# The order of the FFN's first products, of two heads' products, and of layer 1's modulation in a two-layer diffusion trunk

## The chip, the cores and the metric

The kernel runs on one core of one Trainium2 chip. The metric is the device time of one execution in microseconds. Three runs of the kernel before took 2241.53, 2242.65 and 2244.84 us.

## The reference

One inference step of a trunk with two layers, on 128 context tokens and 512 latent tokens of width 1024, everything in float32. A layer is

```python
mod = silu(cond) @ w_mod + b_mod                       # six vectors of 1024: sh1, sc1, g1, sh2, sc2, g2
h = rms_norm(x) * (1 + sc1) + sh1
a = w_out(merge(neighbourhood attention, grouped-query attention, gated linear attention)(h))
x = x + g1 * a
h = rms_norm(x) * (1 + sc2) + sh2
u = h @ ffn_w_up                                       # 1024 -> 2 x 2816
a, g = split(conv3(u));  x = x + g2 * ((a * silu(g)) @ ffn_w_down)
```

The context tokens use the modulation of `c_ctx`, the latent tokens that of `c`. In the gated linear attention each head's output is a product inside the block plus two products (forward and backward) with the state before the block.

## The kernel before, in words

**Layout.** Activations lie channel-major: a tile is 128 channels by 640 tokens (128 context, 512 latent), and a product runs on halves of 320 tokens (`HT`), called left and right. A float32 product is made of three products of rounded parts, hi·hi, hi·lo and lo·hi, so each operand is split into a hi part (a rounding copy, mostly on ScalarE) and a lo part (a subtraction on VectorE or GpSimd). Weights come from HBM in the order of a plan, through SyncE's queue, and are split in the same way.

**The planner.** The program is a set of Python generators ("streams"). Each yields what it waits for; `Order` keeps an estimated clock for each engine, and always steps the first stream in order of priority that is ready at PE's estimated time, else the one that is ready soonest. So the order of each engine's instructions is fixed when the kernel is built. Priority 0 is for evacuations, factors, splits and weights, 1 for attention and modulation, 2 for the main stream that issues the large products. 

**Buffers.** Most working tiles come from one pool `ub` of 49 tiles of 128×648 (in the mixers four more, which `widen` hands to the weights before the output projection). A stream that asks for a tile waits until one is free. In the FFN the pool holds the factors (28 tiles), two half-tiles `a_hi` and `a_lo` for each finished unit until the part's last down chunk, `up_a`, `up_g` and `cv_a` of the units in work, and `w_last` for each pair of weights in preparation. PSUM gives the products six banks of 512 columns.

**The FFN.** There are 22 units of 128 channels; a unit needs the two up projections a and g. Units 0 and 1 are computed from unnormalised input while the norm is still being made (`raw`, tile `up`). Units 2 to 21 use a seven-product scheme of Strassen's kind over the two halves of tokens and the two up matrices: the normalised input of each of four block pairs gives seven factors, B11 and B21 (right columns), B22 (left), and the differences T1 to T4, each as hi and lo (`factors`). A unit's products go in steps "12" (with B11, B21), "67" (T2, T3), "54" (T1, T4) and "3" (B22), into PSUM tiles pair_x, pair_y and pair_w (`pair_step`); "6" goes into the bank that "1" was read from. `pair_act` adds them up, convolves and gates, and `keep_split` makes a_hi and a_lo.

The down projection runs in five parts of 5, 5, 5, 4 and 3 units (`FFN_PARTS`), each in eight chunks of 128 output channels, "dn". The order of all these steps is made by `ffn_steps`: a part's first chunk is put three steps after the "3" of its last unit (`WAIT`), and then one chunk after each step. A chunk runs one half of the tokens over all units and then the other half (`proj_halves`); each half is evacuated into x with the gate.

**The modulation.** Each of the six vectors is a product of `cT` (32 columns) with 1024×1024 weights, read in 256 KB pieces. `Mod.rest` takes five tiles of `ub`, when eight are free, four of them a ring of two slots; a round loads two blocks of rows (four DMAs, 1 MB), makes eight products of 32 columns by 256, and adds the result to a partial sum. Layer 0's last four vectors run in its mixer, with at least 4000 ns of PE's estimated time between rounds. Layer 1's six vectors, 24 rounds, start when the event `calm` is set, which is at the start of branch b's gates ("gb") in layer 0, at priority 1 and with 2000 ns.

**Gated linear attention.** `gla` is called for two pairs of heads in each layer. Its last products go into one PSUM tile `go`, for each block of 128 tokens and each head: v times At (128 rows), and, but for the context block, two products with the states (64 rows, tiles `S` and `qt`).

Of the kernel before, what the change touches and what calls it, by code (L numbers as in the profile page):

```python
# [9 lines left out]
F32 = mybir.dt.float32  # L10
# [8 lines left out]
P = 128  # L19
D = 1024  # L20
KC = 8
# [243 lines left out]
class Order:  # L265
# [105 lines left out]
def kernel(ctx: ExitStack, tc: tile.TileContext, I, O, depth=2):  # L371
# [358 lines left out]

    class Mod:
        def __init__(self, l, pc=None, ready=None):
            self.l, self.pc, self.ready = l, pc, ready
# [36 lines left out]
            del acc  # L770
            yield from self.finish(ms, pieces, P, 256)

        def rest(self, vectors, after, pause):
# [14 lines left out]
            fetch(0)  # L788
            fetch(1)
            for i in range(0, len(todo), 2):  # L790
                v, k0 = todo[i]
                yield ring[0] + ring[1] + [cT, od.later(pause)]
                acc = yield from TB("mod")
                psum_names.add(acc.ap.tensor.name)
# [4 lines left out]
                yield [acc]  # L799
                if k0 == 0:  # L800
                    act(ms[:, :256], acc[:, :256])
                else:
                    tt(ms[:, :256], acc[:, :256], ms[:, :256], ADD)
                del acc
# [110 lines left out]
        h.done[k].time = od.known[lo.ap.tensor.name]  # L915


    def factors(fa, fb, out, k):

        L, R = slice(0, HT), slice(HT, NT)  # L920
        h1, l1, h2, l2 = yield from ub.several("f_12", 4, 0, F32R)
        b11, b12, b21, b22 = fa[:, R], fa[:, L], fb[:, R], fb[:, L]

        def lo(nm, x, h, l):
            tt(l, x, h.bitcast(F32), SUB, sooner(HT))
            out[nm][k] = (h, l)
            out[nm].ready[k].time = od.known[l.tensor.name]

        yield [fa]
        act(h1[:, L], b11)  # L930
        yield [fb]
        act(h1[:, R], b21)
        act(h2[:, L], b22)
        yield [h1]
        lo("B11", b11, h1[:, L], l1[:, L])
        lo("B21", b21, h1[:, R], l1[:, R])
        yield [h2]
        lo("B22", b22, h2[:, L], l2[:, L])

        yield [fb]  # L940
        tt(b22, b22, b12, SUB)
        tt(b12, b12, b11, SUB)
        tt(b11, b22, b11, ADD)
        tt(b21, b21, b11, SUB)
        yield [fa]
        act(h2[:, R], b12)
        h3 = yield from U("f_hi", F32R)
        act(h3[:, L], b11)
        yield [h2]
        lo("T1", b12, h2[:, R], l2[:, R])  # L950
        l3 = yield from U("f_lo", F32R)
        yield [h3]
        lo("T2", b11, h3[:, L], l3[:, L])
        act(h3[:, R], b21)
        h4 = yield from U("f_34", F32R)
        act(h4[:, L], b22)
        yield [h3]
        lo("T4", b21, h3[:, R], l3[:, R])
        yield [h4]
        lo("T3", b22, h4[:, L], h4[:, R])  # L960
        out.keep += [h1, l1, h2, l2, h3, l3, h4]

    class Factors:
        def __init__(self, nk):
# [26 lines left out]
                   skip_group_check=True)  # L991

    def modulate_factors(x, r, mod, i, offs, out):
        gsc, sh = mod.gsc[:, i], mod.T[:, 24 * i:24 * i + 8]
        cols = [(slice(a, a + n), slice(offs[e], offs[e] + n), e) for e, (a, n) in enumerate(((0, NP), (NP, NS)))]
        for k in range(KC // 2):
            f = []
            for kk in (k, k + KC // 2):
                yield [r, mod.have[12 * i + 4 + kk // 2], mod.have[12 * i + kk // 2]]
                v = yield from U("hv")  # L1000
                eng = sooner(NT)
                for c, o, e in cols:
                    tt(v[:, c], x[kk][:, c], r[:, o], MUL, eng)
                yield [v]
                for c, _, e in cols:
                    act(v[:, c], v[:, c], AF.Identity, scale=gsc[:, kk, e:e + 1], bias=sh[:, kk, e:e + 1])
                f.append(v)
                del v
            od.start(factors(f[0], f[1], out, k), 0)
            del f  # L1010


    def scaled(x, k, ready, mod, i, gh, gl, done):
# [74 lines left out]
    def gla(l, p, q, k, rc, v, zT, zdone, wg, pc, oc, grp):  # L1088
# [198 lines left out]
        for ts_ in ((0,), (1, 2, 3, 4)):  # L1287
# [1 line left out]
            psum_names.add(op.ap.tensor.name)  # L1289
            yield At + qts + [v]  # L1290
            for c, t in enumerate(ts_):
                for h in range(2):
                    r = slice(64 * h, 64 * h + 64)
                    oo = op[r, c * P:(c + 1) * P]
                    mm(oo, v[:, t * P + 64 * h:t * P + 64 * h + 64], At[h][:, t * P:(t + 1) * P], True, t == 0)
                    if t:
                        for e in range(2):
                            mm(oo, sst[e][r, t - 1], qts[e][r, t * P:(t + 1) * P], False, e == 1)
# [387 lines left out]
    def mixer(l, h, pc, wg, raws, full, finish, calm):  # L1686
# [416 lines left out]
        z = yield from pair_act(i, c, pc, ah)  # L2103
        yield from keep_split(i, z, ah, al, have)

    def ffn(l, x, raws, h, pc, mod, ss, nxt, nraws):
        ah, al = {}, {}
        have = [Event() for _ in range(NFF)]
        pairs = {}
# [11 lines left out]
        for step in ffn_steps():  # L2121
# [77 lines left out]
    def program():  # L2199
# [20 lines left out]
        for l in range(depth):  # L2220
# [3 lines left out]
            if l == 0:  # L2224
                yield [h.done[0]]
            if l == 0:
                od.start(mod.rest((2, 3, 4, 5), mod.have[3], 4000.0), 1)
            nxt = None
            if l + 1 < depth:
                nxt = Mod(l + 1)  # L2230
            od.start(next_mod(nxt, calm), 1)
            od.start(spill(x, h.done[KC - 1]), 1)
            full, x = [Event() for _ in range(KC)], [None] * KC

# [21 lines left out]
                ss, nraws = SumSq(), Raw()  # L2256
            else:
                ss = nraws = None
            yield from ffn(l, x, raws, h, pc, mod, ss, nxt, nraws)
            raws = nraws  # L2260
            if nxt is not None:
                mod, pc, wg = nxt, nxt.pc, nxt.wg
# [1 line left out]
    def next_mod(nxt, after):  # L2264
        yield [after]
        if nxt is not None:
            nxt.pc, nxt.wg, nxt.ready, work = load_params(nxt.l)
            od.start(work, 1)
            yield from nxt.rest(range(6), after, 2000.0)

    def spill(x, ready):
        yield [ready]
# [65 lines left out]
```

## Time and profile before

| | |
|---|---|
| median of three runs | 2242.65 us |
| profiled execution, its span | 2246.69 us, 2244.9 us |
| PE busy | 2129.1 us, 95% |
| VectorE (DVE) busy | 1565.5 us, 70% |
| ScalarE (ACT) busy | 1124.9 us, 50% |
| mean granted clock of PE | 0.978 |
| DMA | 209.33 MB, mean 93 GB/s |

The profile is of one execution. A row of the timeline has the start, the time to the end of the last instruction, the engine, the line, the operation, the tile written and the tiles read, and how many instructions it merges; a float32 product with `cT`, `At` or `qt` shows as two instructions, one with rounded operands as one. Products overlap, so the time from one row's start to the next one's start is the better measure of their pace. Layer 0's mixer ends and its FFN begins at 715 us, layer 1 begins at 1178 us, its FFN at 1781 us.

### The profile page before, as it was taken

To read this page: it belongs to the slowest core of one execution; us is meant where nothing else is said; L and a number is where in the kernel's file an instruction comes from. 1 tells how busy PE (TensorE), PEld (TensorE's weight loads), DVE (VectorE), ACT (ScalarE), POOL (GpSimd) and SP (SyncE) were. 2 spreads that over 40 slices of the span, in tenths; PEclk is the share of its full clock that TensorE was granted. 3 is DMA by queue.
4 is the path that set the end of the run, shared out by engine and by line. 5 is a ranking of instruction groups with operands and counts; after the bars stand their busy time and mean duration, and the time that the engine had idled before them with its cause. 6 is when DMAs were issued, how large, how long until landed. Compare 5 with 4: busy or idle time off the path is not lost. (4 is left out here: it accounts for less than half of the span.)

```text
span 2244.9 us, 40057 instructions
## 1 busy us (share of the span) xinstructions
PE 2129.1 (95%) x16208; PEld 2002.3 (89%) x16208; DVE 1565.5 (70%) x2839; ACT 1124.9 (50%) x2067; POOL 222.5 (10%) x284
## 2 busy tenths in 40 slices
PE   6999999999999899999998999999999989999999
PEld 4767989896799789999998889899899978999999
DVE  5375479774247987777876865787655798778785
ACT  4354656552225744454456556565543574445452
POOL 0211110000101000001011110101010200000101
PEclk9998999999999999999999899999999999999999
DMA  9751221126662122222223111211113212222212
GB/s 300 259 189 39 68 80 52 38 72 197 218 205 76 38 73 87 80 78 81 69 83 113 49 51 65 78 53 48 39 49 131 76 38 73 88 85 69 92 62 90
DMA packets 85874, 209.33 MB, mean 93 GB/s; under 512 B 9590, under 2 KB 22518, under 8 KB 85688
## 3 DMA queue, kind: packets, MB, share of 16 engines
q1 hardware_dynamic: 84472, 204.66, 28.0%
q8 instruction: 128, 2.10, 0.4%
q0 software_dynamic: 1216, 2.10, 0.3%
q14 instruction: 58, 0.48, 0.1%
HBM read 197.81 MB, written 10.98 MB: 93 GB/s over the span
## 5 line engine op out<-in xcount | busy, mean ns | idle before, releaser
L445 ACT ACTIVATE w_h<-w_st 128x1024 fp32r<-128x1024 f32 (+4 forms) x292 | 274.3, 942 | 246.7 <-PE dn L436 76.7
L461 DVE TENSOR_TENSOR w_h<-w_st,w_h 128x1024 fp32r<-128x1024 f32 (+4 forms) x248 | 269.0, 1087 | 142.1 <-ACT w_h L445 139.3
L436 PE MATMUL dn<-a_hi,w_h 128*128 128x320 f32 x1408 | 325.6, 313 | 2.4 <-ACT a_hi L445 2.0
L436 PE MATMUL pair_x<-f,w_h 128*128 128x320 f32 x1440 | 232.2, 312 | 23.8 <-ACT f L445 18.1
L436 PEld LDWEIGHTS dn<-a_hi,w_h 128*128 128x128 f32 x1408 | 242.0, 191 | 4.0 <-ACT a_hi L445 4.0
L436 PEld LDWEIGHTS pair_x<-f,w_h 128*128 128x128 f32 x1440 | 217.4, 190 | 27.1 <-ACT f L445 18.6
L436 PE MATMUL dn<-a_lo,w_h 128*128 128x320 f32 x704 | 221.1, 314 | 16.8 <-DVE a_lo L461 16.8
L464 POOL TENSOR_TENSOR w_h<-w_st,w_h 128x1024 fp32r<-128x1024 f32 (+2 forms) x44 | 98.5, 2239 | 746.2 <-ACT w_h L445 585.9
L436 PEld LDWEIGHTS dn<-a_lo,w_h 128*128 128x128 f32 x704 | 134.2, 191 | 19.0 <-DVE a_lo L461 18.7
L473 DVE SCALAR_TENSOR_TENSOR x<-dn,modT,x 128x128 f32<-128x128 f32 (+2 forms) x240 | 97.5, 436 | 53.5 <-PE dn L436 53.1
L436 PE MATMUL gc<-h_hi,w_h 128*128 128x320 f32 x512 | 130.4, 325 | 0.0
L436 PE MATMUL ga<-h_hi,w_h 128*128 128x320 f32 x512 | 128.0, 320 | 0.2 <-ACT sg L445 0.2
L436 PE MATMUL gb<-h_hi,w_h 128*128 128x320 f32 x512 | 128.1, 320 | 0.0
L436 PE MATMUL wo<-m_hi,w_h 128*128 128x320 f32 x768 | 113.8, 310 | 0.0
L436 PEld LDWEIGHTS wo<-m_hi,w_h 128*128 128x128 f32 x768 | 113.1, 188 | 0.4 <-issue 0.4
L436 PEld LDWEIGHTS gb<-h_hi,w_h 128*128 128x128 f32 x512 | 88.9, 189 | 7.5 <-issue 7.5
L436 PEld LDWEIGHTS gc<-h_hi,w_h 128*128 128x128 f32 x512 | 89.9, 192 | 5.2 <-issue 2.0
L436 PEld LDWEIGHTS ga<-h_hi,w_h 128*128 128x128 f32 x512 | 89.6, 191 | 2.9 <-issue 2.4
L445 ACT ACT_TABLE_LOAD x63 | 80.8, 1283 | 10.7 <-PE hss L436 2.7
L436 PE MATMUL gc<-h_lo,w_h 128*128 128x320 f32 x256 | 80.3, 314 | 0.0
L436 PE MATMUL ga<-h_lo,w_h 128*128 128x320 f32 x256 | 79.9, 312 | 0.0
L436 PE MATMUL gb<-h_lo,w_h 128*128 128x320 f32 x256 | 79.6, 311 | 0.0
(411 smaller groups left out, 5328.2 us busy)
## 6 DMA issues: line engine op xcount, KB each, us to landing
w_st<-in_wt_dram SPq DMA_DIRECT2D x204, 512.0 KB, 3.5
mod<-in_w_mod_dram SPq DMA_DIRECT2D x160, 256.0 KB, 4.1
w_st<-in_wt_dram SPq DMA_DIRECT2D x48, 320.0 KB, 2.8
mod_w<-in_w_mod_dram SPq DMA_DIRECT2D x32, 256.0 KB, 6.0
xd<-x SPq DMA_DIRECT2D x16, 320.0 KB, 6.7
x<-xd SPq DMA_DIRECT2D x16, 320.0 KB, 3.0
w_st<-in_wt_dram SPq DMA_DIRECT2D x16, 256.0 KB, 2.6
w_st<-in_wt_dram SPq DMA_DIRECT2D x16, 192.0 KB, 2.3
```

The lines of the kernel that those rows point to most:

```text
L436: nc.tensor.matmul(out, lhsT, rhs, start=start, stop=stop, **kw)
L445: r = nc.scalar.activation(out=out, in_=in_, func=f, **kw)
L461: nc.vector.tensor_tensor(out, a, b, op=op)
L464: nc.gpsimd.tensor_tensor(out, a, b, op=op)
L473: nc.vector.scalar_tensor_tensor(out=out, in0=a, scalar=s, in1=b, op0=op0, op1=op1)
```

## The change

1. `ffn_steps` puts "12" of units 2 and 3 first, then "67" and "54" of unit 2, "67" of unit 3 and "3" of unit 2; from unit 4 on the weave is as it was.
2. `modulate_factors` makes the right columns of all eight blocks and their factors B11 and B21 first (`right_factors`), then the left columns and the other factors (`left_factors`, which makes T3 and T2 before T1 and T4). The blocks' tiles `hv` stay until then.
3. The first down chunk of each part runs both halves for each unit (`proj_whole`), not half after half, and evacuates both at the end.
4. `gla` takes the two heads in turn for each of a block's three products.
5. Layer 1's modulation starts after branch b's attention is done, at priority 3, below the main stream, and without a pause; when part 1 of layer 0's down chunks begins, `hurry` lifts it to priority 1 and gives it a pause of 2000 ns. Its vectors gather in PSUM over eight blocks of rows, and are copied out once.

```diff
@@ ffn_steps
-    for n in range(NRAW, NFF + 1):
-        up, last = n < NFF, n > NRAW
+    a, b = NRAW, NRAW + 1
+    weave += [("12", a), ("12", b), ("67", a), ("54", a), ("67", b), ("3", a)]
+    for n in range(NRAW + 2, NFF + 1):
+        up, last = n < NFF, True
@@ Order
+    def lift(self, gen, prio):
+        for s in self.streams:
+            if s[2] is gen:
+                s[0] = prio
+        self.streams.sort(key=lambda s: s[:2])
@@ Mod.rest
-                yield ring[0] + ring[1] + [cT, od.later(pause)]
-                acc = yield from TB("mod")
+                yield ring[0] + ring[1] + [cT, od.later(self.pause)]
+                if k0 == 0 or not whole:
+                    acc = yield from TB("mod")
...
-                           j == 0, j == 1, tile_position=(0, 32 * g))
+                           k0 + j == a, k0 + j == b, tile_position=(0, 32 * g))
...
+                if not whole or k0 == KC - 2:
+                    yield [acc]
+                    if whole or k0 == 0:
+                        act(ms[:, :256], acc[:, :256])
@@ factors
+    def right_factors(fa, fb, out, k):
+        h, l = yield from ub.several("f_12", 2, 0, F32R)
+        for nm, x, c in (("B11", fa, L), ("B21", fb, R)):
+            yield [x]
+            act(h[:, c], x[:, R])
+            yield [h]
+            factor_lo(out, k, nm, x[:, R], h[:, c], l[:, c])
+        out.keep += [h, l]
+    def left_factors(fa, fb, out, k):
...
+        h2, l2 = yield from ub.several("f_12", 2, 0, F32R)
...
+        out.keep += [h2, l2, h3, l3, h4]
@@ modulate_factors
+        for cols, then in zip(sides, (right_factors, left_factors)):
+            for k in range(KC // 2):
...
+                od.start(then(v[k], v[k + KC // 2], out, k), 0)
+                if then is left_factors:
+                    v[k] = v[k + KC // 2] = None
@@ gla
-                for h in range(2):
-                    r = slice(64 * h, 64 * h + 64)
...
+                for j in range(3 if t else 1):
+                    for h in range(2):
+                        r = slice(64 * h, 64 * h + 64)
+                        oo = op[r, c * P:(c + 1) * P]
+                        if j == 0:
+                            mm(oo, v[:, t * P + 64 * h:t * P + 64 * h + 64], At[h][:, cols], True, t == 0)
+                        else:
+                            mm(oo, sst[j - 1][r, t - 1], qts[j - 1][r, cols], False, j == 2)
@@ mixer
-            if nm == "b":
-                calm.time = 0.0
...
                 if nm == "b" and i == 0:
                     od.start(last.serve(mmb, 4), 0)
+                    calm.time = 0.0
@@ ffn
+                if part == 1:
+                    rush.time = 0.0
...
-                yield from proj_halves(w, a, nb, finish(o, part), "dn")
+                if o:
+                    yield from proj_halves(w, a, nb, finish(o, part), "dn")
+                else:
+                    ps, ev = (yield from proj_whole(w, a, nb, HT, "dn")), finish(o, part)
+                    for hf in range(2):
+                        od.start(ev(hf, ps.pop(0)), 0)
@@ program
-            od.start(next_mod(nxt, calm), 1)
+            lazy = next_mod(nxt, calm)
+            od.start(lazy, 3)
...
+    def hurry(mod, lazy, when):
+        yield [when]
+        mod.pause = 2000.0
+        od.lift(lazy, 1)
```

## Rows read from the trace of the kernel before

**Rows 1.** The page's first part: busy us (share of the span) and instructions by engine.

```profile
PE 2129.1 (95%) x16208; PEld 2002.3 (89%) x16208; DVE 1565.5 (70%) x2839; ACT 1124.9 (50%) x2067; POOL 222.5 (10%) x284
```

**Rows 2.** PE's waits, whole span: waiter, releaser, us in total, times, longest.

```profile
PE pair_x L436 <- ACT f L445: 18.1, 2, 9.0
PE dn L436 <- DVE a_lo L461: 16.8, 8, 2.6
...
PE dn L436 <- ACT a_hi L445: 2.0, 2, 1.0
```

**Rows 3.** PE's timeline, second gla: start us, us, instruction, how many.

```profile
239.18 0.43 PE L436 MATMUL go<-At,vc 128*64 128x128 f32 x2
239.54 0.65 PE L436 MATMUL go<-qt,S 64*64 64x128 f32 x4
240.12 0.43 PE L436 MATMUL go<-At,vc 128*64 128x128 f32 x2
```

**Rows 4.** PE's timeline, first gla.

```profile
185.48 0.69 PE L436 MATMUL go<-At,vc 128*64 128x128 f32 x2
...
187.14 0.69 PE L436 MATMUL go<-At,vc 128*64 128x128 f32 x2
```

**Rows 5.** PE's timeline, one unit of the grouped-query attention.

```profile
401.31 0.44 PE L436 MATMUL g_o<-gp,gcv 128*64 128x128 f32 x4
401.58 1.04 PE L436 MATMUL g_o<-gp,vbT 128*64 128x128 f32 x16
402.56 0.42 PE L436 MATMUL ga<-h_hi,w_h 128*128 128x320 f32 x1
```

**Rows 6.** PE's timeline, waits before first down chunks (in brackets: idle before, releaser).

```profile
820.93 0.63 PE L436 MATMUL dn<-a_lo,w_h 128*128 128x320 f32 x1 [2.61 <-DVE a_lo L461]
...
2173.11 0.42 PE L436 MATMUL dn<-a_lo,w_h 128*128 128x320 f32 x1 [1.39 <-DVE a_lo L461]
```

**Rows 7.** PE's timeline, layer 0's FFN between two parts.

```profile
904.24 1.92 PE L436 MATMUL pair_w<-f,w_h 128*128 128x320 f32 x12
906.00 0.74 PE L436 MATMUL pair_x<-f,w_h 128*128 128x320 f32 x4
```

**Rows 8.** PE's waits between 700 and 860 us.

```profile
PE pair_x L436 <- ACT f L445: 9.0, 1, 9.0
...
PE pair_x L436 <- DVE w_h L461: 1.5, 3, 1.0
PE pair_x L436 <- DVE f L461: 1.3, 1, 1.3
PE dn L436 <- ACT a_hi L445: 1.0, 1, 1.0
```

**Rows 9.** Busy us by stage: window, length, PE, PEld, DVE, ACT, POOL, clock, DMA.

```profile
724.00:821.00 97.00, 81.46 (x529) 79.35 (x527) 92.33 (x166) 64.38 (x117) 7.12 (x14) 0.94 0.18 60
```

**Rows 10.** VectorE's timeline, the in-place differences of one block pair.

```profile
733.54 2.07 DVE L461 TENSOR_TENSOR hv<-hv 128x320 f32<-128x320 f32 x4
```

**Rows 11.** Layer 1's modulation: its instructions (ns min/median/max, first and last start), its stage.

```profile
L436 PE MATMUL mod<-mod,cT x384: 376/379/404, 507.0 to 660.2; 128*32 128x256 f32 x192
L501 SPq DMA_DIRECT2D mod<-in_w_mod_dram x92: 327/366/1021, 507.7 to 653.5; - x92
...
DMA to landing us min/median/max: 2.8/3.9/5.9
...
505.00:665.00 160.00, 38.71 (x396) 13.05 (x396) 7.64 (x18) 2.31 (x6) 0.99 0.66 212
```

**Rows 12.** PE's products of tiles gb and bb in both layers, first and last start.

```profile
L436 PE MATMUL gb<-h_hi,w_h x256: 302/309/616, 505.9 to 649.1; 128*128 128x320 f32 x128
...
L436 PE MATMUL bb<-ob_hi,w_h x128: 304/309/421, 597.6 to 657.4; 128*128 128x320 f32 x128
...
L436 PE MATMUL gb<-h_hi,w_h x256: 302/309/415, 1616.3 to 1717.1; 128*128 128x320 f32 x128
...
L436 PE MATMUL bb<-ob_hi,w_h x128: 303/308/315, 1675.0 to 1724.1; 128*128 128x320 f32 x128
```

More of the change, by code (lines that the diff above doesn't have):

```diff
@@ L732, in __init__ @@
         def __init__(self, l, pc=None, ready=None):
-            self.l, self.pc, self.ready = l, pc, ready
+            self.l, self.pc, self.ready, self.pause = l, pc, ready, 0.0 if l else 4000.0
             self.T = prm.tile([P, 48, 2], F32, tag="modT", bufs=2, name=f"modT{l}")
@@ L771, in first, with rest @@
             yield from self.finish(ms, pieces, P, 256)
-        def rest(self, vectors, after, pause):
+        def rest(self, vectors, after, whole):
             yield [after]
@@ L791, in rest @@
                 v, k0 = todo[i]
-                yield ring[0] + ring[1] + [cT, od.later(pause)]
-                acc = yield from TB("mod")
-                psum_names.add(acc.ap.tensor.name)
+                yield ring[0] + ring[1] + [cT, od.later(self.pause)]
+                if k0 == 0 or not whole:
+                    acc = yield from TB("mod")
+                    psum_names.add(acc.ap.tensor.name)
+                a, b = (0, KC - 1) if whole else (k0, k0 + 1)
                 for j in range(2):
@@ L797, in rest @@
                         mm(acc[32 * g:32 * g + 32, :256], cT[:, k0 + j, :], ring[j][g // 2][:, g % 2 * 256:g % 2 * 256 + 256],
[L798 to L804 removed]
+                           k0 + j == a, k0 + j == b, tile_position=(0, 32 * g))
[4 more added lines that the diff above has]
+                    else:
+                        tt(ms[:, :256], acc[:, :256], ms[:, :256], ADD)
+                    del acc
                 for j in range(2):
@@ L915, in mod_lo @@
         h.done[k].time = od.known[lo.ap.tensor.name]
-    def factors(fa, fb, out, k):
-        L, R = slice(0, HT), slice(HT, NT)
-        h1, l1, h2, l2 = yield from ub.several("f_12", 4, 0, F32R)
-        b11, b12, b21, b22 = fa[:, R], fa[:, L], fb[:, R], fb[:, L]
[L924 to L930, printed above, removed]
+    L, R = slice(0, HT), slice(HT, NT)
@@ new lines, in factor_lo @@
+    def factor_lo(out, k, nm, x, h, l):
+        tt(l, x, h.bitcast(F32), SUB, sooner(HT))
+        out[nm][k] = (h, l)
+        out[nm].ready[k].time = od.known[l.tensor.name]
+    def right_factors(fa, fb, out, k):
[6 more added lines that the diff above has]
+        out.keep += [h, l]
@@ L941, in factors @@
         tt(b22, b22, b12, SUB)
+        h4 = yield from U("f_34", F32R)
+        act(h4[:, L], b22)
         tt(b12, b12, b11, SUB)
         tt(b11, b22, b11, ADD)
-        tt(b21, b21, b11, SUB)
-        yield [fa]
-        act(h2[:, R], b12)
         h3 = yield from U("f_hi", F32R)
         act(h3[:, L], b11)
+        tt(b21, b21, b11, SUB)
+        l3 = yield from U("f_lo", F32R)
+        yield [h4]
+        lo("T3", b22, h4[:, L], h4[:, R])
+        yield [h3]
+        lo("T2", b11, h3[:, L], l3[:, L])
@@ L949, in factors @@
+        act(h2[:, R], b12)
+        act(h3[:, R], b21)
         yield [h2]
         lo("T1", b12, h2[:, R], l2[:, R])
[L951 to L956, printed above, removed]
         yield [h3]
         lo("T4", b21, h3[:, R], l3[:, R])
-        yield [h4]
-        lo("T3", b22, h4[:, L], h4[:, R])
-        out.keep += [h1, l1, h2, l2, h3, l3, h4]
+        out.keep += [h2, l2, h3, l3, h4]
@@ L994, in modulate_factors @@
         gsc, sh = mod.gsc[:, i], mod.T[:, 24 * i:24 * i + 8]
[L995 to L1010, printed above, removed]
+        n = HT - NP
+        sides = (((slice(HT, NT), slice(offs[1] + n, offs[1] + NS), 1),),
+                 ((slice(0, NP), slice(offs[0], offs[0] + NP), 0), (slice(NP, HT), slice(offs[1], offs[1] + n), 1)))
+        v = [None] * KC
+        for cols, then in zip(sides, (right_factors, left_factors)):
+            for k in range(KC // 2):
+                for kk in (k, k + KC // 2):
+                    yield [r, mod.have[12 * i + 4 + kk // 2], mod.have[12 * i + kk // 2]]
+                    if v[kk] is None:
+                        v[kk] = yield from U("hv")
+                    eng = sooner(HT)
+                    for c, o, e in cols:
+                        tt(v[kk][:, c], x[kk][:, c], r[:, o], MUL, eng)
+                    yield [v[kk]]
+                    for c, _, e in cols:
+                        act(v[kk][:, c], v[kk][:, c], AF.Identity, scale=gsc[:, kk, e:e + 1], bias=sh[:, kk, e:e + 1])
+                od.start(then(v[k], v[k + KC // 2], out, k), 0)
+                if then is left_factors:
+                    v[k] = v[k + KC // 2] = None
     def scaled(x, k, ready, mod, i, gh, gl, done):
@@ L1291, in gla @@
             for c, t in enumerate(ts_):
-                for h in range(2):
-                    r = slice(64 * h, 64 * h + 64)
[L1294 to L1298, printed above, removed]
+                cols = slice(t * P, (t + 1) * P)
+                for j in range(3 if t else 1):
[6 more added lines that the diff above has]
+                            mm(oo, sst[j - 1][r, t - 1], qts[j - 1][r, cols], False, j == 2)
             n = P * len(ts_)
@@ L2104, in pair_split, with ffn @@
         yield from keep_split(i, z, ah, al, have)
-    def ffn(l, x, raws, h, pc, mod, ss, nxt, nraws):
+    def ffn(l, x, raws, h, pc, mod, ss, nxt, nraws, rush):
         ah, al = {}, {}
@@ L2142, in ffn @@
                     a = [ah.get(k) for k in ks], [al.get(k) for k in ks]
-                yield from proj_halves(w, a, nb, finish(o, part), "dn")
+                if o:
+                    yield from proj_halves(w, a, nb, finish(o, part), "dn")
+                else:
+                    ps, ev = (yield from proj_whole(w, a, nb, HT, "dn")), finish(o, part)
+                    for hf in range(2):
+                        od.start(ev(hf, ps.pop(0)), 0)
+                    del ps, ev
                 if o == KC - 1:
@@ L2226, in program @@
             if l == 0:
-                od.start(mod.rest((2, 3, 4, 5), mod.have[3], 4000.0), 1)
+                od.start(mod.rest((2, 3, 4, 5), mod.have[3], False), 1)
             nxt = None
@@ L2258, in program @@
                 ss = nraws = None
-            yield from ffn(l, x, raws, h, pc, mod, ss, nxt, nraws)
+            rush = Event()
+            if nxt is not None:
+                od.start(hurry(nxt, lazy, rush), 1)
+            yield from ffn(l, x, raws, h, pc, mod, ss, nxt, nraws, rush)
             raws = nraws
@@ L2268, in next_mod @@
             od.start(work, 1)
-            yield from nxt.rest(range(6), after, 2000.0)
+            yield from nxt.rest(range(6), after, True)
+    def hurry(mod, lazy, when):
+        yield [when]
+        mod.pause = 2000.0
+        od.lift(lazy, 1)
     def spill(x, ready):
```

7 lines of the change are left out of this document (2 added, 5 removed).

## The prediction

> **What bounds the kernel now.** I read the page's busy shares first: TensorE (PE) works 2129.1 of 2244.9 us [rows 1], so a change pays where it shortens PE's own work or one of the waits that make up the other 115.8 us. The view of PE's waits names two that belong to the FFN: the pair products on a factor (18.1 us, two waits) and the down products on the newest half (16.8 and 2.0 us) [rows 2]. I then read PE's timeline at each place that the diff touches, because a busy PE can also work slowly: in the heads' products it does. Last come the stage table around the first FFN's head, for what stands behind its waits, and the views of layer 1's modulation.
>
> **Base of the sum.** The profiled execution took 2246.69 us, 1.8 more than its span; the median shown is 2242.65, 4.0 less. I sum against the execution and take the 4.0 off at the end.
>
> **Heads' turns (gla).** Now a head's three products for one block follow each other, so each accumulates behind the last in the same rows: from one head's At product to the other's is 240.12 − 239.18 = 0.94 us, 1.88 a block [rows 3]. The grouped attention already alternates two heads of the same 128×64 shape: its ten products stand from 401.31 to 402.56, so 0.25 a pair [rows 5]. Three alternated pairs make 0.75 a block, 1.13 less; four blocks with an inter-block part give 4.5 an instance, and three of the four instances run so: 13.6. The first runs at half clock: 187.14 − 185.48 = 1.66 a head, 3.32 a block [rows 4]; at twice 0.75 it saves about 1.8 a block, 7.3, of which I keep 6.4, since the block order is the only thing changed and its wait on qt stays. Together −20. Nothing hides this: PE is the busy engine on both sides. The trace has no two 64-row products of different heads in one PSUM bank, so I bound them by the rows: alternating only the At pairs saves 2×0.36 − 0.25 = 0.47 a block at full clock and about 0.74 at half, −8.6 in all.
>
> On that point a rule speaks against the change. The Trainium skill, page "TensorEngine Tiling (Array Packing)", section "Restrictions and Gotchas", says that different row tiles cannot access one PSUM bank at the same time. Both heads write one bank, though other partitions of it; by the rule only the lower bound would come, −8.6. No row shows the case; it is rival 3.
>
> **First down chunk of each part with both halves.** With the halves in turn, PE has 12 products (0.147 each: 12 in 906.00 − 904.24 = 1.76 us [rows 7]) before it needs the part's last half-tile; with both halves together it has 24, so 1.76 more cover. Eight of the ten parts wait: 3.65 in part 0 of each layer (1.04 on a_hi and 2.61), 1.39 in one, and the other five (16.8 − 2×2.61 − 1.39)/5 = 2.04 [rows 2, 6]. Each loses what the cover reaches: 7×1.76 + 1.39 = −13.7. Bounds: 0, if the half-tile comes later by as much, and the 18.8 of rows 2. It takes two PSUM banks at once of six; three are held by pairs at that point, so I cost it at nothing.
>
> **Right factors and products first.** The first FFN waits 9.0 + 1.3 on unit 2's last factor [rows 8]. The right factors need one column half and no differences, so "12" of units 2 and 3 can follow the raw columns directly, 3.5 us of PE work more before it stands. But VectorE works 92.33 of the 97 us from the first factor to the last half-tile of part 0 [rows 9], and none of its work goes: the four in-place differences of a pair still take 2.07 [rows 10], and each block's first product is cut in three pieces instead of two, eight more instructions a layer. What PE gains early it gives back to VectorE before the first down chunk. At most the idle 4.7 comes back; at worst the eight pieces cost 0.52 each, 4.1. I take −2.5 for each of the two FFNs, −5.
>
> **Layer 1's modulation, taken away where it stood.** It is 24 rounds of eight products; PE is busy with them 38.71 us, 1.61 a round [rows 11]. From the first gb to the last bb layer 0 takes 657.4 − 505.9 = 151.5, layer 1, which has no modulation there, 1724.1 − 1616.3 = 107.8 [rows 12]. The difference and the last round, which stands behind bb, make −45.
>
> **... and put where it goes.** At priority 3 it advances only when nothing else can. Layer 1's same stretch has no PE wait up to the FFN's head, so it will start there: one step takes five tiles of the pool `ub` (if eight are free) and fetches. About ten tiles should be free, the raw columns' sixteen having just come back. Rows 8 show six waits and rows 6 a seventh, the longest good for two rounds, and a tighter pool adds a few: I take ten rounds in waits that are there anyway, at +5 in all (0 to 16).
>
> It keeps the five tiles until its last round. The pool has 49 in the FFN. At step ("67", 7), with part 0's chunks half done, the code must hold 28 factor tiles (7 for each of four block pairs), 10 half-tiles of units 0 to 4 (freed only by the eighth chunk), 2 each of units 5, 6 and 7 (up_a and up_g of unit 7 must exist before "1" is read, which "6" waits for), and unit 7's w_last: 45. With five gone there are 44. So the main stream should stand still there until the modulation has run out, one round after the other, and PE with it; queued behind it are ("67", 7) and everything after, and ScalarE and VectorE run dry. A round then lasts as long as its data: a ring slot is fetched when its half of the products is through, 0.8, two issues of 0.37, landing 3.9 (median) [rows 11], which is 5.4; as the other slot's products overlap a little I take 5.2. Bounds: 4.3 with the shortest landing, 2.8, and 6.4, the spacing they have now ((660.2 − 507.0)/24). Fourteen rounds (9 to 19) make 73, with 3 for products at half clock afterwards: +76 (42 to 125). If the pool is too tight at the head, `hurry` starts it in part 1 and the same count binds in part 2, for about the same price.
>
> The fewer evacuations (18 VectorE additions go) are worth nothing: VectorE has room there.
>
> Sum: −20 − 13.7 − 5 − 45 + 5 + 76 = −2.7; 2246.69 − 2.7 − 4.0 = 2240.0. About what a measurement of this kernel can tell from no change is 0.2%, 4.5 us: the forecast is no change, gains eaten by one standstill.
>
> **Rivals.**
> 1. The five tiles never bind: a unit gets by with fewer, or the modulation takes its tiles so late that no five-unit part follows. For: the last parts hold 8 and 6 half-tiles, 43 or fewer. Against: the count, and 24 rounds need over 100 us. Then the rounds cost 24×1.61 = 38.6 and some 5 of waits on data, less 8 in idle places, +36 instead of +81: 2195.
> 2. Slower: the standstill in part 0 lasts longer, 17 rounds at 6.4, 109 and 3, with 3 for the rest: −83.7 + 115 = +31, 2274. For: rounds now come 6.4 apart, with weights on the same queue. Against: in a standstill nothing else is fetched. It decides from the point where the standstill passes 79 us, 15 rounds at 5.2.
> 3. By the skill's rule the heads overlap in the At pairs alone: 11.4 less gain, 2251. For: no row shows the case. Against: the heads write other partitions.
> 4. The change does not do what it says at the down chunks: VectorE, 92.33 of 97 busy before part 0, shifts the last half-tile with PE, and no cover is gained: 2254. Against: in the parts after it PE alone is full.
>
> **Numbers.** Forecast 0.42, with a range of its own of 2220 to 2262; rival 1 0.28, rival 2 0.16, rival 3 0.08, rival 4 0.06. The forecast's own spread (rounds and their price) is 0.45 below the 0.2% bound, 0.25 within it, 0.30 above. So faster is 0.28 + 0.19 + 0.01 = 0.48; same 0.11 + 0.04 = 0.15; slower 0.37. The range that leaves out two in ten reaches rival 1 below and nearly rival 2 above: 2190 to 2272.
>
> **What would show it.** Right: in gla, pairs of products 0.25 apart and go some 3.5 us long; first chunks waiting under 0.5 us in parts 1 to 3; in layer 0's FFN, between part 0's fifth chunk and its end, a stretch of 60 to 90 us with PE idle on mod loads and nothing else running, at the low one of the two clock levels (1.2 GHz); layer 1's FFN shorter by about 10 us. Wrong: rounds of modulation spread through parts 1 to 3 between full-speed products (rival 1, some 45 us faster), 64-row products still 0.29 apart (rival 3), or an FFN head whose factor wait is gone with VectorE no fuller than now, by which my bound on that edit falls.

## The result: 2256.43 us, 0.6% slower than before

The changed kernel takes 2256.43 us (2252.57 to 2258.47, four runs) against 2242.84 beside it: a ratio of 1.0055, 95% interval 1.0042 to 1.0067. The forecast was 2240, no change. The span of its profiled execution is 2256.7 us, 11.8 more than before. The page after, in its busy shares and in 40 slices of 56 us, shows two places:

```profile
PE 2129.3 (94%) x16208; PEld 1989.5 (88%) x16208; DVE 1564.8 (69%) x2837; ACT 1127.9 (50%) x2082; POOL 216.9 (10%) x285
...
PE   6989999999997968999999899999999979999999
...
PEclk9999999999997998999999999999999989999999
DMA  9751221112323374222223212211114202232222
```

PE's busy time has not moved [rows 1] although its heads' products are shorter, so something else became longer. Slices 13 and 15 (PE 7 and 6) are the first FFN's head and the end of its part 0. Slices are counted from 1. I cut each trace at the first products of the FFN and of layer 1, as in these rows of after (first and last start us):

```profile
L445 PE MATMUL up<-xg_hi,w_h x128: 303/310/553, 656.6 to 686.0; 128*128 128x322 f32 x128
...
L445 PE MATMUL qc<-xg_hi,w_h x32: 307/311/316, 1205.6 to 1214.3; 128*128 128x322 f32 x32
...
L445 PE MATMUL up<-xg_hi,w_h x128: 305/311/553, 1801.0 to 1830.5; 128*128 128x322 f32 x128
```

| us | to layer 0's FFN | that FFN | layer 1's mixer | to the end | span | ratio (interval) |
|---|---|---|---|---|---|---|
| before | 715.5 | 462.1 | 603.2 | 464.1 | 2244.9 | |
| after | 656.6 | 549.0 | 595.4 | 455.7 | 2256.7 | 1.0055 |
| moved | -58.9 | +86.9 | -7.8 | -8.4 | +11.8 | |
| forecast, by its terms | -55.9 | +71.5 | -9.1 | -9.2 | -2.7 | |
| e1 turns | 700.4 | 462.1 | 596.2 | 463.9 | 2222.6 | 0.9908 (0.9895 to 0.9922) |
| e2 first chunk | 715.9 | 451.8 | 600.7 | 456.8 | 2225.2 | 0.9908 (0.9895 to 0.9922) |
| e3 right first | 713.7 | 463.3 | 596.0 | 465.8 | 2238.8 | 0.9957 (0.9944 to 0.9969) |
| e4 modulation last | 669.7 | 531.8 | 595.6 | 463.4 | 2260.5 | 1.0075 (1.0063 to 1.0088) |
| e5 all but right first | 656.5 | 526.4 | 584.7 | 454.8 | 2222.4 | 0.9933 (0.9919 to 0.9947) |
| e6 all, four tiles | 652.9 | 512.4 | 584.8 | 456.0 | 2206.1 | 0.9850 (0.9830 to 0.9870) |
| e7 all but modulation | 705.5 | 452.2 | 588.0 | 456.3 | 2202.0 | 0.9805 (0.9787 to 0.9822) |
| e8 e5 with four tiles | 651.7 | 508.7 | 585.5 | 455.1 | 2201.0 | 0.9829 (0.9813 to 0.9845) |
| e9 all, five tiles, late | 652.2 | 523.0 | 587.9 | 455.7 | 2218.8 | 0.9894 (0.9881 to 0.9908) |
| e10 all, two tiles, late | 651.2 | 494.2 | 595.8 | 457.0 | 2198.2 | 0.9825 (0.9811 to 0.9839) |
| e11 e10, old factors | 655.9 | 490.3 | 593.4 | 455.3 | 2194.9 | 0.9791 (0.9774 to 0.9808) |
| e12 turns, first chunk | 699.5 | 451.2 | 593.8 | 455.1 | 2199.6 | 0.9818 (0.9801 to 0.9835) |

The stretches are those of one profiled execution of each kernel; the ratio is of all its runs to the kernel before, run beside it. Gains in us that are given from ratios below are that share of 2246.69. FFN stretches that no edit touches repeat within 0.7 us (464.1, 463.9 and 463.4 for layer 1's in before, e1 and e4). The stretch ahead of layer 0's FFN does not: no edit is made to what stands before the first gla, and that begins between 180.5 and 186.9 us.

All the loss is in layer 0's FFN. Of its 86.9 us, 81.2 are one stop. The modulation's instructions from 650 to 900 us, what PE waited for before them, and who waited for them:

```profile
L445 PE MATMUL mod<-mod,cT x384: 376/403/637, 703.4 to 880.1; 128*32 128x256 f32 x192
...
  DMA mod<-in_w_mod_dram: 28.6, 32
...
  POOL up_a L2077: 97.1, 1
```

The last row is the lock: the memset on GpSimd that opens a new unit's tile `up_a` waits 97.1 us, once, for modulation products, because the tile that it was given is one that the modulation held. PE's timeline shows where (a round is 16 recorded instructions, two for each product):

```profile
799.81 1.07 PE L445 MATMUL mod<-mod,cT 128*32 128x256 f32 x16
803.89 0.63 PE L445 MATMUL mod<-mod,cT 128*32 128x256 f32 x4 [3.02 <-DMA mod<-in_w_mod_dram]
805.14 4.60 PE L445 MATMUL mod<-mod,cT 128*32 128x256 f32 x20 [0.62 <-DMA mod<-in_w_mod_dram]
...
881.01 0.69 PE L450 MATMUL modt<-cn,mod 128*128 128x128 f32 x2 [0.54 <-ACT mod L454]
```

PE runs nothing but the modulation from 799.81 to 881.01; the other engines are nearly dry (window, length, PE, PEld, VectorE, ScalarE, GpSimd, clock, DMA share, GB/s):

```profile
800.00:881.00 81.00, 52.26 (x312) 12.39 (x304) 2.30 (x19) 1.97 (x6) 2.78 (x5) 0.85 0.75 239
```

That is the forecast's standstill at its place, with 19 rounds at 81.2/19 = 4.27 us instead of 14 at 5.2. Most of what else was not forecast lies at that FFN's head: from the first up product to the first down product, at 773.3, it takes 116.7 us, before 814.9 - 715.5 = 99.4. There PE waits five times on left factors:

```profile
695.09 0.41 PE L445 MATMUL pair_x<-f_lo,w_h 128*128 128x320 f32 x1 [1.14 <-DVE f_lo L470]
...
697.58 0.63 PE L445 MATMUL pair_x<-f_hi,w_h 128*128 128x320 f32 x1 [1.93 <-ACT f_hi L454]
702.56 0.64 PE L445 MATMUL pair_x<-f_lo,w_h 128*128 128x320 f32 x1 [4.35 <-DVE f_lo L470]
...
703.40 1.94 PE L445 MATMUL mod<-mod,cT 128*32 128x256 f32 x16
706.18 0.64 PE L445 MATMUL pair_x<-f_hi,w_h 128*128 128x320 f32 x1 [0.85 <-ACT f_hi L454]
708.41 0.63 PE L445 MATMUL pair_x<-f_lo,w_h 128*128 128x320 f32 x1 [1.60 <-DVE f_lo L470]
```

They come to 9.87 us, where one wait of 9.05 and one of 1.30 stood [rows 8]; PE's clock meanwhile is granted at the lower of its levels, 1.2 GHz (0.50 of full speed), and VectorE has no free time:

```profile
700.00:710.00 10.00, 4.99 (x25) 2.97 (x26) 9.83 (x23) 2.18 (x5) 0.20 (x2) 0.50 0.36 120
```

The down products' waits did go, from 16.8 and 2.0 us in both layers [rows 2] to 2.8, and the heads' products take about half their time. A block of two heads is now 1375.83 - 1374.87 = 0.96 us, before 1.88 [rows 3], where 0.75 was forecast:

```profile
1374.87 0.44 PE L445 MATMUL go<-At,vc 128*64 128x128 f32 x4
1375.24 0.65 PE L445 MATMUL go<-qt,S 64*64 64x128 f32 x8
1375.83 0.44 PE L445 MATMUL go<-At,vc 128*64 128x128 f32 x4
```

### The profile page after: what moved, and what is told of

Read it like the earlier page. It is cut to its first block, busy times and chain, and to the rows that moved or that the text cites. A ratio compares the mean times of both kernels' runs of the same rounds, so it can differ in the third digit from the quotient of the medians.

```text
span 2256.7 us, 40079 instructions
## 1 busy us (share of the span) xinstructions
PE 2129.3 (94%) x16208; PEld 1989.5 (88%) x16208; DVE 1564.8 (69%) x2837; ACT 1127.9 (50%) x2082; POOL 216.9 (10%) x285
## 5 line engine op out<-in xcount | busy, mean ns | idle before, releaser
L470 DVE TENSOR_TENSOR w_h<-w_st,w_h 128x1024 fp32r<-128x1024 f32 (+4 forms) x254 | 274.9, 1084 | 130.0 <-ACT w_h L454 124.0
L445 PE MATMUL dn<-a_hi,w_h 128*128 128x320 f32 x1408 | 319.9, 309 | 0.0
L473 POOL TENSOR_TENSOR w_h<-w_st,w_h 128x1024 fp32r<-128x1024 f32 (+3 forms) x38 | 83.3, 2192 | 499.2 <-ACT w_h L454 316.4
L445 PE MATMUL gb<-h_hi,w_h 128*128 128x320 f32 x512 | 122.5, 314 | 0.0
L445 PE MATMUL mod<-mod,cT 128*32 128x256 f32 x640 | 85.7, 445 | 34.8 <-DMA mod<-in_w_mod_dram 33.2
L445 PEld LDWEIGHTS mod<-mod,cT 128*32 128x32 f32 x640 | 22.5, 116 | 89.4 <-DMA mod<-in_w_mod_dram 79.1
L445 PE MATMUL pair_x<-f_hi,w_h 128*128 128x320 f32 x320 | 80.7, 319 | 8.8 <-ACT f_hi L454 7.4
```

Source lines behind the costliest of these rows:

```text
L445: nc.tensor.matmul(out, lhsT, rhs, start=start, stop=stop, **kw)
L470: nc.vector.tensor_tensor(out, a, b, op=op)
L473: nc.gpsimd.tensor_tensor(out, a, b, op=op)
```

## Experiments

**The four parts alone (e1 to e4).** Each is the kernel before with one part of the diff: in e1 the heads' loop, in e2 the first chunk, in e3 the order of the factors and of the first products, in e4 all that touches the modulation.

```
e1  +                for j in range(3 if t else 1):
    +                    for h in range(2):
e2  +                    ps, ev = (yield from proj_whole(w, a, nb, HT, "dn")), finish(o, part)
e3  +    weave += [("12", a), ("12", b), ("67", a), ("54", a), ("67", b), ("3", a)]
    +        for cols, then in zip(sides, (right_factors, left_factors)):
e4  +            lazy = next_mod(nxt, calm)
    +            od.start(lazy, 3)
    ...
    +            yield from nxt.rest(range(6), after, True)
```

> Before, with the heads' turns in gla alone. Theory (the whole change's trace shows both kinds of products of tile go at half their old busy time, 19.8 instead of 40.9 us in all): nothing gives it back, 17 to 20 us faster, about 2225, with the gain in both gla stretches of each layer. Rival: the At, qt and merge work of VectorE behind it is late instead, and half of it comes back as a wait: 2233 or more.

2224.38 us: 0.92% less is 20.7 us on the profiled execution. The theory holds; the gain is in both layers, 15.1 us ahead of layer 0's FFN and 7.0 in layer 1's mixer. More than the turns shows in the first gla, which ran at the lower clock level in the kernel before [rows 4]. In e1 it runs at the higher one, though its wait on qt is as long as before (2.08 us, before 2.10). The same 10 us in before and then in e1, and e1's pace of a block there, 188.44 - 187.49 = 0.95 us:

```profile
190.00:200.00 10.00, 10.00 (x38) 7.03 (x37) 1.12 (x2) 2.78 (x6) 0.00 (x0) 0.50 0.07 28
```

```profile
190.00:200.00 10.00, 10.00 (x124) 9.05 (x120) 4.83 (x8) 8.35 (x14) 0.00 (x0) 1.00 0.18 54
...
187.49 0.44 PE L436 MATMUL go<-At,vc 128*64 128x128 f32 x4
...
188.44 0.44 PE L436 MATMUL go<-At,vc 128*64 128x128 f32 x4
```

> Before, with each part's first down chunk whole alone. Theory (the added cover of 1.76 us reaches nearly all of each wait, and where PE no longer stops its clock does not fall): the 18.8 us of PE's waits on a_lo and a_hi fall below 4, 13 to 17 us faster, about 2228. Rival (VectorE delivers the last half-tile as much later as PE comes earlier in part 0 of each layer, 7.3 us of the waits stay): 2234.

2226.27 us, also 20.7 less, more than either theory gave, though 7.9 us of the waits stay, near the rival's 7.3. The two FFNs give 10.3 and 7.3, of which 10.9 are waits. In layer 0 the clock gives most of the rest: after the waits of 3.65 us before part 0's first chunk PE worked on below full clock, and for as many products PE's busy time in that FFN falls from 440.3 to 435.7 us (in layer 1's from 438.9 to 438.2). Kernel before, then e2, same window, then e2's waits:

```profile
815.00:830.00 15.00, 11.36 (x59) 10.86 (x58) 8.61 (x15) 6.06 (x12) 2.48 (x3) 0.77 0.08 22
```

```profile
815.00:830.00 15.00, 12.84 (x87) 12.57 (x87) 13.85 (x23) 8.03 (x13) 0.20 (x2) 1.00 0.11 31
```

```profile
PE dn L436 <- DVE a_lo L461: 7.9, 8, 2.2
```

87 products instead of 59 are done in the same 15 us.

> Before, with the right factors and products first alone. Theory (VectorE is full from the first factor to part 0's down chunk, PE only comes earlier to the same shortage and meets it in five short waits on f_hi and f_lo instead of one long one, at half clock between them): 2 to 4 us slower for each FFN, about 2249. Rival (the prediction's): 2.5 us faster for each FFN, 2238. In the first case the waits of pair products stay above 10 us for each FFN and the stretch from the last up product to the first down product grows from 69.6 to about 73.

2234.95 us, 9.7 less: by the total it looks like the rival. The stretches say otherwise: the FFNs are 1.2 and 1.7 us longer, PE's waits on f_hi and f_lo in layer 0's come to 11.2 us, and from the last up product to the first down product it takes 74.3 us there and 72.8 in layer 1, before 69.9. 7.2 us come from layer 1's mixer, which this part does not touch. Its order of instructions came out differently when the kernel was built, without a wait of 7.0 us of tile `kc` on its weights. Of the fourteen kernels seven have that wait (6.7 to 7.0 us) and are the longer ones there: 600.7 and 603.2 against 595.6 and 596.0 with the heads as before, 593.4 to 596.2 against 584.7 to 588.0 with the turns.

> Before, with layer 1's modulation moved alone. Theory (a standstill on the five tiles that it holds, 19 of 24 rounds at 4.3 us, the rest at the FFN's head at 2 to 3 us each): 49 us off before the FFN, 81 and some 10 to 14 on in it, 40 to 46 slower, about 2286. Rival (the standstill needs the new factor order's longer hold of its tiles): rounds spread through the FFN, 5 to 10 faster, 2235.

2262.32 us, 16.8 more. The rival falls, and the theory's counts too: this is the prediction's own picture, ten rounds before the standstill and 14 in it. The first five run in the place of the 9-us wait, from 700.27 to 719; the standstill is 812.61 to 873.9, 4.4 us a round:

```profile
700.27 1.07 PE L442 MATMUL mod<-mod,cT 128*32 128x256 f32 x16
...
812.61 1.07 PE L442 MATMUL mod<-mod,cT 128*32 128x256 f32 x16
816.64 0.63 PE L442 MATMUL mod<-mod,cT 128*32 128x256 f32 x4 [2.97 <-DMA mod<-in_w_mod_dram]
...
873.49 0.44 PE L447 MATMUL modt<-cn,mod 128*128 128x128 f32 x2 [0.54 <-ACT mod L451]
```

But the ten are not nearly free: the way from the first up product to the first down product is 786.0 - 669.7 = 116.3 us, before 814.9 - 715.5 = 99.4. That is 16.9 for ten. The four parts alone sum to 34 us faster, together they are 14 slower, so they do not add. Between the profiled executions the gap is 44 us: 26.3 lie in layer 0's FFN, where parts clash, and 16.5 in layer 1's mixer, where e3 and e4 gained by its order and the whole change has the slow one.

**Which two (e5), and is it the tiles (e6, e8).** e5 is the changed kernel with the factors and their products as before. e6 keeps four tiles, the sums going to a state tile of gla; e8 is both.

```
e6, e8
-            own = yield from ub.several("mod", 5, 3)
-            ms, ring = own[4], (own[0:2], own[2:4])
+            own = yield from ub.several("mod", 4 if self.l else 5, 3)
+            ms = sp.tile([P, 4, HD], F32, tag="S0", ...).rearrange(...) if self.l else own[4]
+            ring = (own[0:2], own[2:4])
```

> The whole change without the right factors first (heads' turns, whole first chunks, modulation last). The four parts alone sum to 34 us faster, together they are 14 slower. Theory: the loss lies between the new factor order and the modulation in layer 0's FFN: with the old order one long wait at the FFN's head holds five rounds and ten are done before part 0's standstill, so 14 rounds and 62 us stand in it as with the modulation alone, not 19 and 81. Then about 20 us faster than before, 2222, with layer 0's FFN (first up product to layer 1's first product) near 521 us. Rival (the whole chunks or the turns are what clashes with the modulation): layer 0's FFN near 549 - 1 and 2250 or more.

2227.55 us, 29 less than the whole change (34 between the profiled executions). Layer 0's FFN is 526.4, 22.6 less, with ten rounds at the head and 14 in the standstill again; another 10.7 come from the mixer's order. So the clash is mainly that of the new factor order with the modulation.

> The whole change, but layer 1's modulation keeps four tiles of the pool instead of five (its sums go to a tile of gla's state that stands idle then). Theory (the standstill in part 0 is a lack of one tile: 45 needed, 44 there): it is gone, PE never sits on modulation loads for more than a few us at part 0's fifth chunk, and rounds run between full-speed products or at part ends: 30 to 60 us faster than the whole change, 2196 to 2226. Rival (the loads themselves or the modulation's place in the priorities make the stop): within 5 us of the whole change, 2256.

2210.39 us, 46 less than the whole change (51 between the profiled executions): 36.6 in layer 0's FFN, 10.6 by the mixer's order. The modulation also starts earlier, since seven free tiles are enough for it, and does seven rounds at the head instead of five. One tile decides the stop: at part 0's fifth chunk, where 19 rounds stood, the stretch is full (first row). A second, shorter stop appears behind the part's last chunk (second row), seven rounds in 29 us:

```profile
790.00:820.00 30.00, 29.89 (x212) 28.85 (x210) 9.63 (x19) 7.03 (x12) 4.33 (x6) 1.00 0.27 90
820.00:850.00 30.00, 21.66 (x116) 5.26 (x116) 16.38 (x31) 7.39 (x13) 0.05 (x1) 0.55 0.71 224
```

> Heads' turns, whole first chunks and the modulation last with four tiles, the factors in their old order. Theory (no standstill at part 0's fifth chunk; eleven rounds at the FFN's head for some 17 us, most others at full speed for 1.6 each): some 10 us faster than with five tiles and the old order at least, 2195 to 2210. Rival (rounds between full-speed products cost what the standstill did, by late factors and down waits): 2222.

2203.26 us, as the theory had it, with the same second stop from 826 to 855. What that one lacks I did not test by itself; with two tiles (e10, e11) it is gone.

**Without the modulation's move (e7), and without the factors too (e12).** e7 is the whole change less what e4 has; e12 is e1 and e2 together.

> The whole change with layer 1's modulation where it was (heads' turns, whole first chunks, right factors first). Theory (the three gains stand on different stretches and add, and only the modulation eats them): 21 and 21 from the first two alone, and of the 10 of the third those 7 that come from another order of layer 1's mixer: 40 to 50 us faster than before, about 2199. Rival (the three share waits and do not add): 25 faster or less, 2220.

> Heads' turns and whole first chunks alone, factors and modulation as before. Beside the version with the right factors first as well (2198.7) it tells what these are worth. Theory (the new factor order gives the FFNs nothing; its gain is that layer 1's mixer comes out in an order without the 6.7 us wait of tile kc on its weights): layer 0's FFN 452 and layer 1's 457 us as with the right factors first, layer 1's mixer some 7 us longer, 595, and 2203 to 2207 in all. Rival (the right factors first save PE waits in the FFN): FFNs 3 us longer each, the mixer the same, 2204 as well, so the stretches decide.

2198.73 and 2202.84 us. Turns and chunks add up: 20.7 and 20.7 alone, 40.9 together. Beside e12, e7's FFNs are 1.0 and 1.2 us longer and its mixer is 5.8 shorter, so the theory of e12 holds: the new factor order gives the FFNs nothing. Ahead of the FFN e7's execution is 6.0 longer: its first gla began 2.1 us later, and products of the modulation waited 13.1 us for their loads there, in e12 8.2. The waits of layer 0's FFN, e7 and then e12, show the exchange:

```profile
PE pair_x L439 <- DVE f_lo L464: 6.8, 3, 4.1
PE pair_x L439 <- ACT f_hi L448: 4.6, 2, 2.7
```

```profile
PE pair_x L436 <- ACT f L445: 9.0, 1, 9.0
...
PE pair_x L436 <- DVE f L461: 1.3, 1, 1.3
```

**The stop at another place, and a version without one (e9 to e11).** e9 lets the modulation begin with part 1, with its five tiles. e10 fetches into two tiles, a half round at a time, from the end of part 0 on; e11 is e10 with the old factor order.

```
e9   -            yield from nxt.rest(range(6), after, True)
     +            yield from nxt.rest(range(6), nxt.rush, True)
e10  +            st = yield from ub.several("mod", 2, 3)
     +            for i, (v, k) in enumerate(todo):
     +                yield st + [cT, od.later(self.pause)]
     ...
     -        mod.pause = 2000.0
     +        mod.pause = 4000.0
```

> The whole change, but the modulation begins only with part 1's first down chunk (none of it at the FFN's head), still with five tiles. Theory (the count of tiles binds at the fifth chunk of any five-unit part that starts while the modulation holds five): no standstill in part 0; 19 rounds run between full-speed products for 1.0 to 1.6 us each in part 1's end and part 2, and the last five stand at part 2's fifth chunk for about 21 us. Layer 0's FFN near 452 + 25 + 21 = 498 us and the whole near 2203. Rival (part 0's stop comes from its place behind the head, not from the tiles held): no run of five rounds with PE idle on their loads in part 2, layer 0's FFN near 480, 2185.

2219.17 us. The place is right: no stop in part 0, and the last five rounds stand in part 2 for 22 us; the memset of `up_a` waits 31.6 us for them:

```profile
1022.17 2.31 PE L445 MATMUL mod<-mod,cT 128*32 128x256 f32 x16
...
1026.16 0.63 PE L445 MATMUL mod<-mod,cT 128*32 128x256 f32 x4 [0.70 <-DMA mod<-in_w_mod_dram]
1028.20 3.00 PE L445 MATMUL mod<-mod,cT 128*32 128x256 f32 x16 [1.42 <-DMA mod<-in_w_mod_dram]
...
1044.44 0.69 PE L450 MATMUL modt<-cn,mod 128*128 128x128 f32 x2 [0.54 <-ACT mod L454]
```

The price of the other 19 was wrong: (523.0 - 452.2 - 22)/19 = 2.6 us each, not 1.0 to 1.6, and part of it is that rounds which follow each other closely wait for their loads (6.3 of the 12.6 us of such waits are among these 19). Another 2.8 us stand in the FFN's head, ahead of the first round: its waits are as in e7, but it takes 105.0 us there and 102.2 in e7.

> The whole change, but the modulation holds two tiles (one fetch at a time, sums in gla's idle state) and is spread from the end of part 0 on, one half round of four products each 4 us of PE's time. Theory (a half round whose data is there costs PE 0.5 us between full-speed products, and nothing stands still): 24 to 30 us for all in place of 46 in the b branch, layer 0's FFN near 480 us and the whole near 2182, below the version with the modulation as before (2199). Rival (each half round waits for its own load of half a megabyte, 2 us or more): 48 such waits, 2270.

> As the version with two tiles, but with the factors in their old order. Theory (right factors first gives the FFN itself nothing, 1 to 2 us slower each, once no rounds stand at its head): 2 to 4 us faster than with the right factors first, about 2179. Rival (the right factors first pay in themselves): 5 or more slower, 2187.

2202.74 and 2195.38 us, 21 and 16 more than the theories gave. No stop, and 0.2 and 0.3 us of waits on loads in all, so the rival of e10 falls. A half round takes 0.57 us from its start to the next product's:

```profile
860.84 0.31 PE L445 MATMUL dn<-a_lo,w_h 128*128 128x320 f32 x1
860.99 0.31 PE L445 MATMUL dn<-a_hi,w_h 128*128 128x320 f32 x1
861.23 0.64 PE L445 MATMUL mod<-mod,cT 128*32 128x256 f32 x8
861.80 0.42 PE L445 MATMUL dn<-a_hi,w_h 128*128 128x320 f32 x1
862.05 0.31 PE L445 MATMUL dn<-a_lo,w_h 128*128 128x320 f32 x1
```

48 of them would be 27, but layer 0's FFN is 42.0 us longer than e7's. The rows show why: the products on both sides of the half round are 0.24 and 0.25 us from the next start, where 0.15 is the pace, so it costs 862.05 - 860.99 - 2 x 0.15 = 0.76 us, 36.5 for 48. Six half rounds take 1.05 to 1.26 instead of 0.57, 3.6 more, and 2.8 stand in the head as in e9, where from 40 to 60 us into the FFN the clock was granted at 0.51, in e7 at 0.66. Together that is 42.9.

What comes off before the FFN is 54.3 against e7 and 43.6 with the old factors (e11 against e12); e4 had 45.8, and e7 was late there by the 6.0 us told above. So without a stop the move is worth 12.3 us by the first pair and 4.5 by the second, and the second is the safer. The mixer's order with the wait, which e10 and e11 got, takes 7.8 of the 12.3 back. The old factor order is again the better one, by 3.9 and 1.7 us in the FFNs, more than its theory's 1 to 2. Of the 4.7 us that e10 is ahead before the FFN, 3.9 are there by the last At product of layer 0's gla, at 229.0 and 232.9 us, where no edit reaches: e10's gla began 2.4 us earlier, and the granted clock from 180 to 220 us was 1.00, in e11 0.96. e11 is the fastest of all kernels here, though its interval overlaps that of e7.

## Why the prediction was wrong

The terms were mostly right in kind, the standstill among them. The step that failed is the price of the rounds at the FFN's head, and with it their number.

- **Heads' turns: right in kind, the size by luck.** -20 forecast, -20.7 alone, but two errors cancel. A pair of At products takes 0.37 us and a 64-row pair 0.29, not 0.25, so a block takes 0.96 and not 0.75, and the three instances at full clock save 11.0, not 13.6. The first was forecast to stay at half clock and save 6.4; in e1 it ran at full clock, a block took 0.95 instead of 3.32, and four blocks save 9.5. Why the clock stayed up there is not shown. Rival 3 falls: the rule that different row tiles cannot access one PSUM bank at once (the Trainium skill, "TensorEngine Tiling (Array Packing)", "Restrictions and Gotchas") would have left the qt products one after the other, and the trace shows eight records of two heads in 1375.83 - 1375.24 = 0.59 us where four of one head took 0.58 [rows 3].
- **First chunk: right in kind, too small.** -13.7 forecast, -20.7 alone, of which the FFNs give 17.6. The term counted waits at their length and left out the slow clock behind the long ones in layer 0, some 4.6 us. Rival 4 falls.
- **Right factors first: the sign of the direct term was wrong.** -2.5 an FFN forecast, +1.0 to +3.9 measured in three pairs of kernels (e3 and before, e7 and e12, e10 and e11). The sentence ahead of it, that VectorE is full there and what PE gains early it gives back, was the right one; PE waits about as long in five pieces (11.4 us in e7 against 10.3).
- **Modulation taken away: right.** -45 forecast, -45.8 in e4.
- **Modulation put in, the standstill: right in cause and place, wrong in count and price.** One tile less held removes it, so the count of 45 against 44 was right to the tile and rival 1 falls; begun later it moves to the next five-unit part. 14 rounds at 5.2 were forecast, 19 at 4.27 came, and the two errors nearly cancel (76 against 81), which is luck. PE's granted clock was 0.85 over the stop, not at the low level throughout as the sign in the prediction had it.
- **Modulation put in, the head: the step that failed.** "I take ten rounds in waits that are there anyway, at +5 in all (0 to 16)." The waits that I counted are those of rows 8, with the old factor order, which another part of the same change removes. With the old order ten rounds do go there (e4, e5), for 16.9 us. With the new one five go, and the head, 116.7 us from first up to first down product, is 14.5 longer than e7's 102.2 and 11.7 longer than the 105.0 of e9 and e10, which have the new order and no round there. So a round costs 2.3 to 2.9 us at the head, not 0.5; with the old order it is 16.9/10 = 1.7. Of the five only the first stands among the waits on factors; the others come after them, and the third and the fourth wait for their own loads:

```profile
712.44 1.69 PE L445 MATMUL mod<-mod,cT 128*32 128x256 f32 x16
716.28 1.66 PE L445 MATMUL mod<-mod,cT 128*32 128x256 f32 x8 [2.15 <-DMA mod<-in_w_mod_dram]
718.55 1.76 PE L445 MATMUL mod<-mod,cT 128*32 128x256 f32 x8 [0.60 <-DMA mod<-in_w_mod_dram]
...
751.25 2.64 PE L445 MATMUL mod<-mod,cT 128*32 128x256 f32 x16 [0.90 <-DMA mod<-in_w_mod_dram]
...
767.22 1.07 PE L445 MATMUL mod<-mod,cT 128*32 128x256 f32 x16
```

  The rounds left over went to the standstill at 4.27. That pieces so short take up few rounds because the order is fixed when the kernel is built, before any real wait is known, fits the traces but was not tried by itself.
- The total missed by 14.5 us: in layer 0's FFN the head took 17.3 where 5 - 2.5 was forecast, 14.8 too much, the standstill 5.2 too much, and its down chunks and the rest 4.6 less than forecast; the other stretches together 0.9 less. Rival 2 (17 rounds at 6.4, 2274) had the sign and not the size. What I had not seen at all is the two orders of layer 1's mixer, worth 5 to 11 us to the kernels here; in the changed kernel the slower one came out, as before.

## What to carry to other kernels

Work that is moved into waits has to be counted against the waits of the changed kernel, not of the old one, and in tiles as well as in time: here giving up one tile of 49 gained 37 us. Where an order is planned when the kernel is built, a part's effect alone contains a share of luck from stretches that it does not touch, so compare by stretches before adding, and only stretches that repeat from one execution to the next. A long wait can cost its length and a slower clock behind it, as before part 0's first chunk in layer 0.

## What the runs showed of the hardware

In the standstill 19 rounds move 1 MB each in 4.27 us. The DMA engines are 75% busy there at 239 GB/s and PE is busy 52.26 of 81.00 us, so neither is full, and a round is as long as the loop of load and products, with the two slots overlapping; which part of it could be shorter was not tried. The 4.27 is near the forecast's lower bound of 4.3, though that was made with a landing of 2.8 us and the modulation's loads took 3.5 in the median. Four 64-row products of two heads, in the two row halves and on other partitions of one PSUM bank, pass in the 0.59 us in which two of one head passed before (0.58). A half round of four products of 32 columns costs 0.76 us between other products, 0.19 more than its own 0.57, at the two changes from one kind of product to the other.
